# Softmax reciprocal of a band-attention layer: from VectorE's reciprocal to GpSimd's power of minus one

## The chip, the cores and the metric

The kernel runs on one core of a Trainium2 chip, in one launch. The metric is device time in microseconds: the median of the timed runs. The engines are named as in the profile: PE is TensorE's matmul, PEld its weight load, DVE VectorE, ACT ScalarE, POOL GpSimd, SP SyncE, whose queue issues most of the DMAs.

## The reference

One inference step of a one-layer streaming encoder, on 2048 prompt tokens and 64 sample tokens of width 1024, all in float32. A modulated RMS norm is followed by one input projection, whose columns feed two mixers: a gated causal convolution of 31 taps over 512 channels, and an attention of 8 heads of 64 in which every chunk of 64 frames reads its own and the 8 chunks before. Both are gated, summed, projected and added to the input; then comes a gated feed-forward of width 2816. The change is in the attention's softmax:

```python
def band_attend(q, k, v, q_pos, k_pos, rel_bias):
    s = jnp.einsum('bqhd,bkhd->bhqk', q, k).astype(jnp.float32) * ATTN_SCALE
    rel = jnp.clip(q_pos[:, None] - k_pos[None, :], -MAX_REL, MAX_REL) + MAX_REL
    s = s + rel_bias[:, rel].astype(jnp.float32)[None]
    ...
    s = jnp.where(mask[None, None], s, NEG_INF)
    p = jax.nn.softmax(s, axis=-1).astype(v.dtype)
    return jnp.einsum('bhqk,bkhd->bqhd', p, v)
```

## The kernel before

Most products are made in three passes: an operand is split into a high part and a low remainder (`hi`, `lo`; `whi`, `wlo` for weights, `hh`, `hl` for the normalised input, `ph`, `pl` for probabilities), and `mm3` (line 700) multiplies high by high, high by low and low by high.

The program has two phases. **Phase 1** (0 to about 1190 us) takes the tokens in four blocks of 576 or 512. For each block it makes q, k and v (stages "q", "k", "v"), then the gated convolution's input and the convolution (stages 0 to 3), then the gates ("g"); the norms of the next block's token tiles are made under the gates. The attention of a block starts after its "v" and runs beside the stages that follow, into the next block. **Phase 2** merges the mixers and runs the feed-forward; the change doesn't touch it.

The convolution's taps are 30 `scalar_tensor_tensor` on DVE for each channel tile and block (line 1252; `y<-u,wd,y` in the profile): output so far plus shifted input times a weight. `conv_norm` (line 1257) then normalises, with sums on POOL (`s<-s,y`, `s<-s,ln`) and a product on POOL (`y<-y,s`).

The attention of one head and block has four score tiles of 128 queries (in the first block there is one more head of 64 sample queries for each head). For a tile, PE multiplies q and k into `sc` (line 1480 or 1491). `softmax_max` (line 1350) lets DVE add the bias, take the row maximum into `sm` column 0 and copy the tile to SBUF (`pr<-sc,bias`); ACT then takes the exponentials in place, with their row sum in `sm` column 2 (`pr<-pr,sm`, and ACTIVATION_READ_ACCUMULATOR). `softmax_scale` (line 1366) makes the sum's reciprocal into `sm` column 3, and ACT multiplies the tile by it (the second `pr<-pr,sm`; `ON_ACT` on line 48 names every block). `attend` (line 1463) issues the scale of tile t-1 behind the maximum of tile t, and the scale of the last tile at the end. PE then transposes the four tiles (`ptp<-ident,pr`), ACT and DVE split the result into `ph` and `pl`, and PE multiplies by v into `po`.

What sets the order. The core's engines run in program order each. The program is written by generators (`attend`, `convolve`, `conv_norm`, `qk_rows`, `norm_tile`) in lanes, which are stepped while PE's products are issued. A small account (class `Stream`, lines 170 to 227) keeps an estimated load for each engine: a step waits until PE's load has reached the load of the engines that it depends on. `stream.after("act", "dve")` raises ACT's load to DVE's less 200 ns, and an operation adds its estimate, 83 ns for the old reciprocal and 260 ns for a power on one column. So a changed estimate moves whole steps between PE's products. A scheduler then places the instructions of each engine.

Beside the softmax, POOL already raises to a power in `rsqrt_mean` (line 722; `r<-t,mhalf`), for the norms: one column for a token tile's norm (`square`, line 1124), eight for the heads' norms of q and k (`qk_rows`). A token tile's norm runs ACT's squares (`junk`), DVE's sum and scale, POOL's power, DVE's product with the tile (`x_t<-x_t,r`), PE's transposes (`pt<-ident,x_t`).

Of the kernel before, what the change touches and what calls it, by code (L numbers as in the profile page):

```python
# [8 lines left out]
F32 = mybir.dt.float32  # L9
F32R = mybir.dt.float32r  # L10
AF = mybir.ActivationFunctionType
ALU = mybir.AluOpType
# [4 lines left out]
P = 128  # L17
# [594 lines left out]
def streaming_layer(ctx: ExitStack, tc: tile.TileContext, I, O):  # L612
    nc = tc.nc
    stream = Stream()
    pe, dve, act, gps = (
        Meter(e, n, stream) for e, n in ((nc.tensor, "pe"), (nc.vector, "dve"), (nc.scalar, "act"), (nc.gpsimd, "pool"))
    )
# [13 lines left out]
    const = ctx.enter_context(tc.tile_pool(name="const", bufs=1))  # L631
# [17 lines left out]
    dve.memset(ones, 1.0 / CONV)  # L649
    mhalf = const.tile([P, 8], F32, name="mhalf")  # L650
    dve.memset(mhalf, -0.5)
    eps_t = const.tile([P, 1], F32, name="eps_t")
    dve.memset(eps_t, EPS)

# [709 lines left out]
        return pr, sm, free, stream.when("act")  # L1364

    def softmax_scale(pr, sm, n, w, on_act):
        dve.reciprocal(sm[:n, 3:4], sm[:n, 2:3])
        if on_act:
            stream.after("act", "dve")
            act.activation(pr[:n, :w], pr[:n, :w], AF.Copy, scale=sm[:n, 3:4])  # L1370
        else:
            dve.tensor_scalar(pr[:n, :w], pr[:n, :w], sm[:n, 3:4], None, ALU.mult)

    def load_qk(x, h, q0, nq, k0, nk):
# [88 lines left out]
    def attend(i):  # L1463
# [10 lines left out]
        for t in range(0, nq, P):  # L1474
            n = min(P, nq - t)
            if x not in (0, "s"):
                ps = ps_a.tile([P, 2, 512], F32, tag="s", name="sc")
                for j in range(2):
                    for d in range(2):
                        pe.matmul(ps[:, j, :320], q2[:, d, t : t + P], kk[:, t + 320 * j : t + 320 * j + 320], start=d == 0, stop=d == 1)  # L1480
                w, src, bs = 640, ps[:, :, :320], bias[:, ::-1]
            else:
                w = nk if x == "s" else t + P

                if "banks" not in now:
                    sc = ps_a.tile([P, 2, 512], F32, tag="s", name="sc")
                    now["banks"] = [sc[:, 0:1], sc[:, 1:2]]
                ps = now["banks"].pop(0)
                now["banks"].append(ps)
                for d in range(2):  # L1490
                    pe.matmul(ps[:n, 0, :w], q2[:, d, t : t + n], kk[:, :w], start=d == 0, stop=d == 1)
                src, bs = ps[:n, 0:1, :w], bias[:n, 64:384][:, ::-1] if x == "s" else bias[:, :w][:, ::-1]
            pr, sm, free, ready = softmax_max(src, n, w, bs)
            tiles.append((pr, sm, n, w))
            if t + P < nq:
                yield free + PE_LAG, SCORE_ROOM
            else:
                fetch(i + 1)
                if (x, order[min(i + 2, len(order) - 1)][0]) in ((0, 0), ("s", "s")):
                    fetch_qk(i + 2)  # L1500
                now["scored"] = i
            if t:
                softmax_scale(*tiles[-2], x in ON_ACT)
        yield ready
        softmax_scale(*tiles[-1], x in ON_ACT)
        yield stream.when("act" if x in ON_ACT else "dve") + PE_LAG
        while now["finished"] < i - 1:
# [747 lines left out]
```

## Time and profile before

| | |
|---|---|
| timed runs | 2988.55, 2989.11, 2995.56 us; median 2989.11 |
| profiled execution | span 2982.2 us from its first to its last instruction; the page gives no other time for it |
| PE, DVE, ACT, POOL busy | 2906.6, 2047.4, 1363.6, 1165.8 us |
| phase 1, 60 to 1190 us | PE idle 28.0 us, DVE busy 850.8 of 1130 us, POOL busy 161.9 us |
| reciprocals of the softmax | 136 on DVE, from 184.4 to 1184.0 us |

How to read it: the page's groups name an instruction by engine, operation, output and inputs with shapes and the number of them, then busy time and mean, then the idle time of the engine before them and what ended it. The view of the waits adds the idle times up by what was waited for. The timeline lists start, duration and instruction, with the idle time ahead of it in brackets. A buffer of four tiles that is used in turn has one name in all of them.

### The profile page before, as it was taken

The numbers are of one execution on the slowest core, as the hardware profiler recorded it, in microseconds if no ns is written. First come the engines' busy times: TensorE is split into PE (matmuls) and PEld (weight loads), VectorE is DVE, ScalarE is ACT, GpSimd is POOL, SyncE is SP. The second block draws the span as 40 slices with busy tenths as digits, with TensorE's granted clock in tenths as the row PEclk, the third lists the DMA queues.
The fourth block names the chain that finished last, engine by engine and source line by source line (L and its number), as shares of the span: only waits on it lengthen the run. The fifth ranks groups of instructions, "written<-read, shape, count | busy, mean of one in ns | idle before, by whom it ended". The sixth has DMA issues, their size and how long they took to land. (4 is left out here: it accounts for less than half of the span.)

```text
span 2982.2 us, 44930 instructions
## 1 busy us (share of the span) xinstructions
PE 2906.6 (97%) x16241; PEld 2588.0 (87%) x16241; DVE 2047.4 (69%) x3628; ACT 1363.6 (46%) x2459; POOL 1165.8 (39%) x752
## 2 busy tenths in 40 slices
PE   7999899999999999989999999999999999999999
PEld 4899777787888888878989899999999999999998
DVE  5897687667857885477677755676666557566666
ACT  3345643662456257464443335544444345444442
POOL 0201310111011102444666443365766742465767
PEclk9999999999999999999999999999999999999999
DMA  8989889888997888885444786423333975333333
GB/s 296 304 282 306 264 286 312 279 256 276 308 283 221 281 256 277 265 284 167 139 147 149 233 268 222 135 89 113 114 106 116 308 244 184 98 96 114 114 104 126
DMA packets 467724, 628.06 MB, mean 211 GB/s; under 512 B 36276, under 2 KB 314664, under 8 KB 467501
## 3 DMA queue, kind: packets, MB, share of 16 engines
q1 hardware_dynamic: 453456, 605.58, 62.8%
q10 hardware_dynamic: 14045, 19.60, 1.9%
q8 instruction: 128, 2.10, 0.3%
q14 instruction: 95, 0.78, 0.1%
HBM read 476.53 MB, written 148.54 MB: 210 GB/s over the span
## 5 line engine op out<-in xcount | busy, mean ns | idle before, releaser
L102 PE MATMUL ps<-t,whi 128*128 128x384 f32 (+1 forms) x2112 | 502.7, 322 | 9.5 <-ACT t L102 4.9
L102 POOL TENSOR_TENSOR wlo<-wst,whi 128x1024 fp32r<-128x1024 f32 (+1 forms) x160 | 365.1, 2292 | 254.1 <-ACT whi L102 231.9
L102 ACT ACTIVATE whi<-wst 128x1024 fp32r<-128x1024 f32 (+1 forms) x264 | 257.4, 977 | 324.8 <-PE ps L102 118.5
L102 PE MATMUL ps<-b,whi 128*128 128x384 f32 (+1 forms) x1584 | 381.3, 326 | 6.1 <-DVE early L102 3.4
L102 PEld LDWEIGHTS ps<-t,whi 128*128 128x128 f32 x2112 | 367.6, 188 | 17.2 <-ACT t L102 5.1
L102 DVE SCALAR_TENSOR_TENSOR y<-u,wd,y 128x512 f32<-128x512 f32 (+1 forms) x480 | 369.1, 773 | 6.4
L102 PE MATMUL ps<-hh,whi 128*128 128x512 f32 (+2 forms) x992 | 361.3, 364 | 0.0
L102 DVE TENSOR_TENSOR acc<-acc,pd 128x512 f32<-128x512 f32 (+1 forms) x482 | 322.5, 685 | 54.9 <-PE pd L102 52.4
L102 PE MATMUL ps<-hl,whi 128*128 128x512 f32 (+2 forms) x992 | 345.2, 348 | 0.0
L102 PE MATMUL ps<-hh,wlo 128*128 128x512 f32 (+2 forms) x992 | 344.9, 348 | 0.0
L102 PE MATMUL ps<-t,wlo 128*128 128x384 f32 (+1 forms) x1056 | 339.3, 321 | 1.0 <-POOL wlo L102 0.7
L102 PE MATMUL pd<-whi,hid 128*128 128x512 f32 (+1 forms) x956 | 307.2, 391 | 0.2 <-DVE hid L102 0.2
L102 PEld LDWEIGHTS ps<-b,whi 128*128 128x128 f32 x1584 | 278.6, 189 | 12.4 <-DVE early L102 4.2
L102 POOL TENSOR_TENSOR r<-t,mhalf 128x1 f32<-128x1 f32 (+3 forms) x68 | 83.7, 1232 | 456.4 <-DVE t L102 451.3
L102 PE MATMUL ps<-b,wlo 128*128 128x384 f32 (+1 forms) x792 | 256.9, 325 | 0.0
L102 ACT ACTIVATE pr<-pr,sm 128x640 f32<-128x640 f32 (+3 forms) x272 | 200.2, 747 | 109.7 <-DVE sm L102 107.1
L102 PEld LDWEIGHTS pd<-whi,hid 128*128 128x128 f32 (+1 forms) x956 | 174.6, 183 | 42.4 <-ACT hid L102 0.7
L102 PEld LDWEIGHTS ps<-hh,wlo 128*128 128x128 f32 x992 | 186.6, 188 | 21.7
L102 PEld LDWEIGHTS ps<-hh,whi 128*128 128x128 f32 x992 | 187.2, 189 | 18.5 <-issue 1.6
L102 PEld LDWEIGHTS ps<-hl,whi 128*128 128x128 f32 x992 | 187.3, 189 | 15.5 <-issue 1.4
L102 PEld LDWEIGHTS ps<-t,wlo 128*128 128x128 f32 x1056 | 198.2, 188 | 2.6 <-POOL wlo L102 1.3
L102 POOL TENSOR_TENSOR wlo<-ws,whi 128x512 fp32r<-128x512 f32 x96 | 125.2, 1325 | 173.7 <-ACT whi L102 170.8
(227 smaller groups left out, 6307.0 us busy)
## 6 DMA issues: line engine op xcount, KB each, us to landing
whi<-w_din_h SPq DMA_DIRECT2D x72, 512.0 KB, 6.6
wlo<-w_din_l SPq DMA_DIRECT2D x72, 512.0 KB, 8.2
wst<-sum_d SPq DMA_DIRECT2D x132, 256.0 KB, 2.8
wfo<-in_w_ffn_out SPq DMA_DIRECT2D x64, 512.0 KB, 3.3
wmod<-in_w_ada SPq DMA_DIRECT2D x46, 512.0 KB, 6.2
sum_d<-ws SPq DMA_DIRECT2D x88, 256.0 KB, 2.4
wst<-in_w_ffn_in SPq DMA_DIRECT2D x84, 256.0 KB, 3.1
wst<-in_w_in SPq DMA_DIRECT2D x40, 512.0 KB, 9.1
```

What stands on the lines that cost most here:

```text
L102: self.last = f(*args, **kw)
```

## The change

A constant column of -1 is made at the start. The reciprocal becomes a power of -1 on GpSimd, and the account of loads follows it: POOL after ACT, then ACT after POOL. ACT still multiplies; the branch for a scale on DVE is not taken by any block.

```diff
     mhalf = const.tile([P, 8], F32, name="mhalf")
     dve.memset(mhalf, -0.5)
+    mone = const.tile([P, 1], F32, name="mone")
+    dve.memset(mone, -1.0)
...
     def softmax_scale(pr, sm, n, w, on_act):
-        dve.reciprocal(sm[:n, 3:4], sm[:n, 2:3])
+        stream.after("pool", "act")
+        gps.tensor_tensor(sm[:n, 3:4], sm[:n, 2:3], mone[:n], ALU.pow)
         if on_act:
-            stream.after("act", "dve")
+            stream.after("act", "pool")
             act.activation(pr[:n, :w], pr[:n, :w], AF.Copy, scale=sm[:n, 3:4])
         else:
+            stream.after("dve", "pool")
             dve.tensor_scalar(pr[:n, :w], pr[:n, :w], sm[:n, 3:4], None, ALU.mult)
```

136 reciprocals leave DVE and 136 powers come to POOL. Apart from the constant, each engine issues the same instructions as before; their order is the same up to the first attention head and again from the end of the last one, and differs between.

First place: POOL at the end of the first block's attention, where the next block's token tiles are normalised. `s<-s,ln` and `y<-y,s` belong to the convolution's norm, `wlo` to a weight, `r<-t,mhalf` 128x1 to a token tile's norm, `sm<-sm,mone` is the new power. Before:

```order
L102 TENSOR_TENSOR s<-s,ln 128x512 x3
L102 TENSOR_TENSOR wlo<-wst,whi 128x1024
L102 TENSOR_TENSOR y<-y,s 128x512 x4
L102 TENSOR_TENSOR r<-t,mhalf 128x1 x2
L102 TENSOR_TENSOR r<-t,mhalf 128x8 x4
```

And now:

```order
L102 TENSOR_TENSOR wlo<-wst,whi 128x1024
L102 TENSOR_TENSOR s<-s,ln 128x512
L102 TENSOR_TENSOR r<-t,mhalf 128x1
L102 TENSOR_TENSOR r<-t,mhalf 128x8
L102 TENSOR_TENSOR y<-y,s 128x512 x4
L102 TENSOR_TENSOR sm<-sm,mone 128x1
L102 TENSOR_TENSOR r<-t,mhalf 128x1
L102 TENSOR_TENSOR sm<-sm,mone 128x1 x2
```

The third token tile's power has moved ahead of the four products, the fourth stands behind them and one softmax power.

Second place: PE at the same point, with the last scores of that block (`sc`) and the fourth token tile's transposes (`pt<-ident,x_t`). Before:

```order
L102 MATMUL sc<-kk,q_1733 128x512 x2
L102 MATMUL ps<-whi,hh 128x512
L102 MATMUL ps<-wlo,hh 128x512
L102 MATMUL ps<-whi,hl 128x512
L102 MATMUL sc<-kk 64x320 x2
L102 MATMUL pt<-ident,x_t 128x128 x4
L102 MATMUL ps<-whi,hh 128x512
```

And now:

```order
L102 MATMUL ps<-whi,hl 128x512
L102 MATMUL sc<-kk,q_1735 128x128 x2
L102 MATMUL sc<-kk,q_1735 128x256 x2
L102 MATMUL sc<-kk,q_1735 128x384 x2
L102 MATMUL sc<-kk,q_1735 128x512 x2
L102 MATMUL pt<-ident,x_t 128x128 x2
L102 MATMUL ps<-whi,hh 128x512
```

The four score tiles now stand together, without products between them, and the sample head comes later.

Third place: DVE at the third head of the second block, from the maximum of its third tile on (ISA is that maximum and its accumulator's reading). Before:

```order
L102 ISA pr,sm<-sc,bias 128x640
L102 ISA sm 128x1
L102 SCALAR_TENSOR_TENSOR y<-u,wd,y 128x512 x2
L102 RECIPROCAL sm<-sm 128x1
L102 SCALAR_TENSOR_TENSOR y<-u,wd,y 128x512
L102 ISA pr,sm<-sc,bias 128x640
L102 ISA sm 128x1
L102 SCALAR_TENSOR_TENSOR y<-u,wd,y 128x512 x2
L102 RECIPROCAL sm<-sm 128x1
L102 SCALAR_TENSOR_TENSOR y<-u,wd,y 128x512 x5
```

And now:

```order
L102 ISA pr,sm<-sc,bias 128x640
L102 ISA sm 128x1
L102 SCALAR_TENSOR_TENSOR y<-u,wd,y 128x512 x4
L102 ISA pr,sm<-sc,bias 128x640
L102 ISA sm 128x1
L102 SCALAR_TENSOR_TENSOR y<-u,wd,y 128x512 x8
```

The reciprocals are gone from between the taps, and the run of taps behind the last tile's maximum has grown to eight.

## The prediction

> **What bounds the kernel now.** The page's first lines, cut to two, give span and PE:
>
> ```profile
> span 2982.2 us, 44930 instructions
> PE 2906.6 (97%) x16241; PEld 2588.0 (87%) x16241; DVE 2047.4 (69%) x3628; ACT 1363.6 (46%) x2459; POOL 1165.8 (39%) x752
> ```
>
> PE is busy for 97% of the span, so another engine matters only where PE waits for it. The view by stretches (start:end, length, busy time of PE, PEld, DVE, ACT, POOL, granted clock, DMA share, GB/s) shows where it can:
>
> ```profile
> 60.00:182.00 122.00, 121.69 (x711) 104.12 (x709) 99.39 (x154) 42.40 (x65) 22.34 (x18) 1.00 0.88 305
> 182.00:430.00 248.00, 231.56 (x1473) 206.51 (x1474) 187.59 (x418) 136.81 (x312) 51.28 (x42) 0.98 0.87 285
> 430.00:1190.00 760.00, 748.73 (x4076) 626.23 (x4075) 563.84 (x1075) 374.61 (x677) 88.32 (x78) 1.00 0.86 276
> 1190.00:2982.00 1792.00, 1766.54 (x9737) 1627.04 (x9735) 1166.00 (x1906) 791.00 (x1370) 999.61 (x600) 1.00 0.51 164
> ```
>
> The last stretch keeps its order and has no softmax. The change can move 182 to 1190 us, where PE is idle for 16.4 and 11.3 us. The waits of PE in phase 1 (total, times, longest) say on what:
>
> ```profile
> PE pt L102 <- DVE x_t L102: 8.9, 4, 5.7
> PE sc L102 <- DVE sm L102: 7.3, 7, 2.3
> PE pm L102 <- POOL s L102: 5.5, 4, 1.9
> PE ptp L102 <- ACT pr L102: 1.4, 3, 0.7
> PE pt L102 <- DVE kn L102: 1.4, 2, 1.2
> ```
>
> The softmax chain reaches PE in two rows: 1.4 us in which transposes wait for the scaled tile (`ptp`), and 7.3 us in which scores wait for a buffer that DVE's maximum frees (`sc`). No gain can be large; a loss has no such lid.
>
> **Term 1, DVE.** What leaves DVE, and what its idle time is worth:
>
> ```profile
> L102 DVE RECIPROCAL sm<-sm x136: 107/157/167, 184.4 to 1184.0; 128x1 f32<-128x1 f32 x128, 64x1 f32<-64x1 f32 x8
> DVE sm L102 <- ACT pr L102: 25.8, 31, 1.5
> ```
>
> 136 x 0.157 = 21.4 us of DVE's work goes, and 25.8 us in which DVE stood before a reciprocal until ACT had the sum. DVE is busy for 187.6 of 248 and 563.8 of 760 us, so nearly all of this is beside PE. On PE it can shorten only the 7.3 us: bounds 0 and -7.3. A score held by the maximum behind one reciprocal gets it 0.16 us sooner, 7 x 0.16: I take **-1.1**.
>
> **Term 2, POOL's time.** The softmax power isn't in this trace, but the norms' power has its size:
>
> ```profile
> L102 POOL TENSOR_TENSOR r<-t,mhalf 128x1 f32<-128x1 f32 x32 | 18.0, 565 | 220.2 <-DVE t L102 219.1 <-DVE sm L102 0.9 <-DMA wst<-in_w_ffn_in 0.2
> ```
>
> 136 x 0.565 = 76.8 us come to POOL, over stretches in which it is busy for 51.3 of 248 and 88.3 of 760 us. Its idle time hides them: **0**, as throughput.
>
> **Term 3, latency of each head's last tile.** Inside a head the scale of tile t-1 stands behind the maximum of tile t, and PE only comes to the transposes later. What counts is the last tile. From its score its chain is maximum, exponential, sum's reading, reciprocal, scale:
>
> ```profile
> L102 DVE CUSTOM_DVE_ANT_0 pr<-sc,bias 128x640 f32<-128x640 f32 x96 | 78.4, 817 | 32.4 <-PE sc L102 30.1 <-DMA bias<-rb_d 1.7
> L102 ACT ACTIVATE pr<-pr,sm 128x640 f32<-128x640 f32 x192 | 156.2, 825 | 65.3 <-DVE sm L102 64.0 <-ACT gate L102 0.4
> L102 ACT ACTIVATION_READ_ACCUMULATOR pr<-pr,sm 128x1 f32 x128 | 23.9, 187 | 0.0
> ```
>
> Without the reciprocal, 0.82 + 0.83 + 0.19 + 0.83 and the maximum's own reading (under 0.1) make about 2.8 us. The reciprocal adds its wait behind DVE's queue; first and last of the 136 pairs, sum's reading and reciprocal:
>
> ```profile
> 182.96 0.19 ACT L102 ACTIVATION_READ_ACCUMULATOR pr<-pr,sm 128x1 f32 x1
> 184.40 0.16 DVE L102 RECIPROCAL sm<-sm 128x1 f32<-128x1 f32 x1
> ...
> 1183.77 0.19 ACT L102 ACTIVATION_READ_ACCUMULATOR pr<-pr,sm 128x1 f32 x1
> 1183.98 0.16 DVE L102 RECIPROCAL sm<-sm 128x1 f32<-128x1 f32 x1 [1.50 <-ACT pr L102]
> ```
>
> End to end the first takes 1.41 us (184.56 less 183.15, a convolution tap in between), the last 0.18; over all 136 the mean is 1.13. An undisturbed power takes 0.57 + 0.05 for the hand-over, 0.62. So the average falls, but the tiles that the taps leave alone get 0.44 us later.
>
> POOL is not always undisturbed. Five of its operations, against like ones (1.65 for the undisturbed eight columns, 0.30 for the 128x64 sum):
>
> ```profile
> 640.62 1.65 POOL L102 TENSOR_TENSOR r<-t,mhalf 128x8 f32<-128x8 f32 x1 [4.01 <-DVE sm L102]
> 919.59 2.02 POOL L102 TENSOR_TENSOR r<-t,mhalf 128x8 f32<-128x8 f32 x1 [6.24 <-DVE t L102]
> 969.48 1.94 POOL L102 TENSOR_TENSOR r<-t,mhalf 128x8 f32<-128x8 f32 x1 [10.60 <-DVE t L102]
> 405.95 2.60 POOL L102 TENSOR_TENSOR r<-t,mhalf 128x8 f32<-128x8 f32 x1 [3.94 <-DVE t L102]
> 354.44 2.62 POOL L102 TENSOR_TENSOR r<-t,mhalf 128x8 f32<-128x8 f32 x1 [2.63 <-DVE t L102]
> 266.66 0.30 POOL L102 TENSOR_TENSOR s<-s,y 128x64 f32<-128x64 f32 x1 [31.58 <-DVE y L102]
> 230.33 4.60 POOL L102 TENSOR_TENSOR s<-s,y 128x64 f32<-128x64 f32 x1 [32.54 <-DVE y L102]
> ```
>
> They were held for 0.37, 0.29, 0.95, 0.97 and 4.30 us, 1.4 in the mean. In the longest hold DVE ran a solid row of operations on two SBUF tensors, and POOL's ended as DVE came to one that reads PSUM (`po`):
>
> ```profile
> 230.88 1.21 DVE L102 TENSOR_TENSOR wlo<-wst,whi 128x1024 fp32r<-128x1024 f32 x1
> 234.77 0.69 DVE L102 TENSOR_TENSOR o_p<-other,po 64x512 f32<-64x512 f32 x1
> ...
> 407.38 0.74 DVE L102 SCALAR_TENSOR_TENSOR y<-u,wd,y 128x512 f32<-128x512 f32 x1
> ```
>
> The tap at 407.38 ran beside the power of 405.95 and kept 0.74 us, so DVE pays nothing that I can see. The Trainium skill says more, in "SBUF — State Buffer", section "Who interferes with whom": a DVE instruction with two SBUF inputs contends with a GpSimd instruction that reads SBUF, and the loser is blocked for the other's whole instruction. By that rule DVE would lose up to 0.565 us for each power that falls into a run of taps, 37.9 us for 67 of them, more than term 1 relieves; the tap at 407.38 doesn't show it, the hold at 230.33 shows POOL's side.
>
> Now each head's margin: in the changed program's order I count PE's products between a head's last score and that tile's transposes, at 0.23 us each for 512 columns (rows 345.86 and 346.09 below), less the reciprocal's latency. Before, 2.2 to 7 us are left, and PE waits 1.4 us in all. Attention steps move in the new order, and distances shrink and grow: the very last head has 2.3 in place of 3.4, so 2.3 - 0.62 = 1.7 are left where 2.8 are needed.
>
> - POOL never held: the shortfalls add to 4.7, less the 1.4 of today: +3.3.
> - Powers that fall in a run of taps (67 of 136 by the order) held 1.4 us: 10.5 - 1.4 = **+9.1**.
> - Powers held until the whole run of taps is over (up to 4.2 us, once 8.8, third head of the second block): 30.1 - 1.4 = +28.7.
>
> I take the middle one, because four of the five holds are under 1 us, and keep both ends.
>
> **Term 4, from block 1 to block 2.** The order shown ahead moves token-tile norms here. Today:
>
> ```profile
> 340.77 0.66 PE L102 MATMUL pt<-ident,x_t 128*128 128x128 f32 x4 [1.29 <-DVE x_t L102]
> ...
> 345.86 0.39 PE L102 MATMUL ps<-wlo,hh 128*128 128x512 f32 x1
> 346.09 0.39 PE L102 MATMUL ps<-whi,hl 128*128 128x512 f32 x1
> ...
> 352.74 1.09 PE L102 MATMUL pt<-ident,x_t 128*128 128x128 f32 x4 [5.65 <-DVE x_t L102]
> ...
> 356.03 0.63 PE L102 MATMUL ps<-wlo,hh 128*128 128x512 f32 x1
> 356.46 0.63 PE L102 MATMUL ps<-whi,hl 128*128 128x512 f32 x1
> ```
>
> ```profile
> 334.80 4.62 POOL L102 TENSOR_TENSOR y<-y,s 128x512 f32<-128x512 f32 x4
> ...
> 351.25 0.55 POOL L102 TENSOR_TENSOR r<-t,mhalf 128x1 f32<-128x1 f32 x1 [11.32 <-DVE t L102]
> ```
>
> PE loses 1.29 + 5.65 = 6.9 us on `x_t`. In the new order the third tile's power leaves its place behind the 4.62 us of products, so the 1.29 should go; the fourth's stands behind those products and a softmax power. I bound the term by 0 (both waits stay) and -6.9 (both go) and take half, **-3.4**. Behind the long wait about ten products stand 0.43 apart and not 0.23, which costs 2.0 us; half of it, **-1**. The Trainium skill has this as the clock gate ("TensorE: Matmul & The Clock Gate", Part 1: half clock after an idle window of about 3.4 us, full after as long a busy one); by its figure a wait of 3.4 us may or may not bring the slow clock, and the trace agrees with its 5.65 us.
>
> **Sum.** -1.1 + 0 + 9.1 - 3.4 - 1.0 = +3.6 us on a span of 2982.2. The median of the runs lies 6.9 us above that span, and I carry this over: 2989.1 + 3.6 = about **2993**.
>
> **Rivals.**
>
> *POOL is blocked through runs of taps* (slower). The mechanism is the 4.30 us hold at 230.33, at each head's last tile. For it: the length of that hold, and POOL's end just as DVE came to a PSUM input. Against it: the four short holds. Price: 28.7 - 1.1 - 3.4 = +24, so 3013. It decides where it takes the sum past +9, so term 3 past 14.5: from +3.3 unheld to +9.1 at a hold of 1.4 us the term grows by 4.1 for each us of hold, so that is a mean hold of about 2.7 us. The skill's sentence above is this rival's rule.
>
> *The reordering alone wins* (faster). Both `x_t` waits and the slow stretch go (-8.9), the `sc` waits go (-7.3), POOL is never held (+3.3): -13, so 2976. For it: those are PE's two largest waits. Against it: most `sc` waits are at a head's start, where no reciprocal is near.
>
> *POOL's own queue*: a last tile's power behind the 4.62 us of products. The order shows powers behind them, none of a last tile, so it costs 1 to 3 us: 2996, within the forecast's range.
>
> That 136 reciprocals don't become 136 powers is excluded by the order.
>
> **How the numbers follow.** The forecast's case is everything within 9 us of the time before, 0.3%, about what a measurement of this kernel can tell from no change: chance 0.60, holding the 2996 as well. The blocked POOL has 0.32, since even half of its price passes 9 us; the winning order 0.08. The range reaches from 2980, part of the way to 2976, to 3013, the slower rival's price: the ends of term 3 with terms 1 and 4 at their bounds.
>
> **What would show it.** Right: powers `sm<-sm,mone` on POOL, 136 with a mean near 1.3 us (0.57 + 1.4 x 67/136); `ptp <- ACT pr` from 1.4 to about 10 us; `pt <- DVE x_t` from 8.9 to about 5; the tap's mean near 0.75. The slower rival: powers with a mean over 1.9 (0.57 + 2.7 x 67/136), `ptp <- ACT pr` near 30. The faster one: `ptp` under 5 with both `x_t` and `sc` near nothing. Taps that grow longer would overturn term 1; a new wait of PE in phase 1 that isn't in these rows, most of all a new place of the four tiles' norms, would overturn term 4.

## The result, and the profile after

The changed kernel takes 3013.16 us (median of 4 runs, 3011.87 to 3013.53) against 2988.83 for the kernel before on the same chip: ratio 1.0076, 95% interval 1.0059 to 1.0092. It is slower by 23 to 24 us, at the upper end of the range and at the price of the rival in which POOL is blocked. The profile shows another mechanism than that rival's. (The ratios of this document leave out one run of the kernel before, 5652 us at a granted clock of 0.936.)

The first lines of the page, after:

```profile
span 3010.1 us, 45010 instructions
PE 2915.1 (97%) x16241; PEld 2588.8 (86%) x16241; DVE 2043.4 (68%) x3493; ACT 1363.7 (45%) x2459; POOL 1248.5 (41%) x888
```

The span is 27.9 us longer than that of before. Nearly all of it lies between the first product of a score and the last product of probabilities with v; cut there, the stretch holds the same number of products in both (before, then after; columns as ahead):

```profile
181.60:1191.00 1009.40, 981.53 (x5556) 833.63 (x5554) 751.77 (x1492) 511.49 (x989) 139.60 (x120) 0.99 0.86 278
183.20:1219.10 1035.90, 994.61 (x5556) 838.16 (x5554) 741.58 (x1356) 512.63 (x988) 222.62 (x256) 0.99 0.84 271
```

The stretch is 26.5 us longer, the rest of the program 1.4. PE's idle time in it goes from 27.9 to 41.3 us, 13.4 more, and the same products keep PE busy for 13.1 us more. Part of this is the clock: by the granted clock in the traces, the stretch runs at half clock for 10.2 us before (two pieces, at 184.7 and 351.9) and for 27.3 us after (five pieces, at 185.7, 195.9, 356.3, 550.9 and 1018.5). One of them:

```profile
550.90:557.70 6.80, 4.02 (x9) 2.70 (x10) 3.36 (x6) 1.19 (x2) 1.24 (x2) 0.50 1.01 313
```

There the products of 512 columns stand 0.43 us apart and not 0.23, as in the prediction's rows. If all take twice their time, 17.1 us more of it costs some 8.5 us (an estimate); the rest of the longer busy time isn't explained here. PE's waits in phase 1, largest first:

```profile
PE ptp L102 <- ACT pr L102: 12.8, 15, 2.0
PE pm L102 <- POOL s L102: 8.0, 4, 4.9
PE sc L102 <- DVE sm L102: 6.4, 11, 1.0
PE pt L102 <- DVE x_t L102: 2.8, 3, 1.3
PE sc L102 <- DMA kk<-k_d: 2.2, 2, 1.6
```

The waits of transposes for a scaled tile have gone from 1.4 to 12.8 us, 3 to 15 of them. By their places in the heads, 11 of the 15 (8.0 us) are at a head's last tile, two (2.7) at a first and two (2.1) at a third. The waits on `x_t` have gone from 8.9 to 2.8; a wait of the convolution's sums (`pm`) has grown to 4.9 us. And the power itself, with what stood before it and who waited for it:

```profile
L102 POOL TENSOR_TENSOR sm<-sm,mone x136: 535/550/1427, 184.8 to 1212.4; 128x1 f32<-128x1 f32 x128, 64x1 f32<-64x1 f32 x8
...
L102 POOL TENSOR_TENSOR sm<-sm,mone 128x1 f32<-128x1 f32 x128 | 80.6, 630 | 403.6 <-ACT pr L102 401.9 <-DMA q<-q_d 1.8
```

```profile
ACT pr L102 <- POOL sm L102: 83.3, 101, 3.1
```

The 128 powers of 128 rows take 0.63 us in the mean; over all 136 the median is 0.55 and the longest 1.43: POOL was not blocked through runs of taps. Pairing each sum's reading with its reciprocal, the mean from the one's end to the other's end even fell, from 1.13 us to 0.87. That mean is held up by a few very late reciprocals before, 13.28 us the latest; the median rose a little, from 0.64 to 0.69. The average latency is better and the kernel slower.

Where it bites is seen in the timelines. First head of the second block, PE before (products left out), then after:

```profile
480.87 0.85 PE L102 MATMUL sc<-kk,q 128*128 128x320 f32 x4 [0.93 <-DVE sm L102]
...
482.75 0.85 PE L102 MATMUL sc<-kk,q 128*128 128x320 f32 x4 [1.03 <-DVE sm L102]
483.44 0.38 PE L102 MATMUL ptp<-ident,pr 128*128 128x128 f32 x2
```

```profile
484.91 0.85 PE L102 MATMUL sc<-kk,q 128*128 128x320 f32 x4 [0.93 <-DVE sm L102]
487.36 0.33 PE L102 MATMUL ptp<-ident,pr 128*128 128x128 f32 x1 [1.60 <-ACT pr L102]
487.45 0.83 PE L102 MATMUL sc<-kk,q 128*128 128x320 f32 x4
```

Before, the first tile's transpose stands behind the third score; after, it stands ahead of it, and PE waits 1.60 us, though DVE's maximum, which the third score needs, ended at 486.62. In blocks 2 to 4 this is the only one of 24 heads in which a transpose stands ahead of the third score. ACT and POOL at that place, after:

```profile
484.89 0.83 ACT L102 ACTIVATE pr<-pr,sm 128x640 f32<-128x640 f32 x1 [0.85 <-DVE sm L102]
485.63 0.19 ACT L102 ACTIVATION_READ_ACCUMULATOR pr<-pr,sm 128x1 f32 x1
486.48 1.55 ACT L102 ACTIVATE pr<-pr,sm 128x640 f32<-128x640 f32 x2 [0.67 <-POOL sm L102]
```

```profile
485.89 0.55 POOL L102 TENSOR_TENSOR sm<-sm,mone 128x1 f32<-128x1 f32 x1 [8.62 <-ACT pr L102]
```

ACT stands idle for 0.67 us while POOL makes the power. What it does first then is the scale, and the next tile's exponential comes behind it (one row, x2). Another head of the same block, ACT before and after:

```profile
616.80 0.83 ACT L102 ACTIVATE pr<-pr,sm 128x640 f32<-128x640 f32 x1 [0.66 <-DVE sm L102]
617.54 0.19 ACT L102 ACTIVATION_READ_ACCUMULATOR pr<-pr,sm 128x1 f32 x1
617.63 0.81 ACT L102 ACTIVATE pr<-pr,sm 128x640 f32<-128x640 f32 x1
```

```profile
629.77 0.82 ACT L102 ACTIVATE pr<-pr,sm 128x640 f32<-128x640 f32 x1
630.49 0.18 ACT L102 ACTIVATION_READ_ACCUMULATOR pr<-pr,sm 128x1 f32 x1
631.40 1.55 ACT L102 ACTIVATE pr<-pr,sm 128x640 f32<-128x640 f32 x2 [0.72 <-POOL sm L102]
```

Before, the exponential (the row with a reading behind it) waits only for its own maximum and the scale of the tile ahead runs behind it, without a wait. After, the scale comes first and waits for its power, and the exponential stands behind both. Counted by start times over the 96 neighbours of the prompt heads, the scale of tile t-1 starts ahead of the exponential of tile t 41 times before and 85 times after. So a power inside a head delays the next tile's exponential, and through it the last tile. From the start of a last tile's maximum to the end of its scale it is 3.65 us in the mean of the 32 prompt heads before and 4.24 after (medians 3.29 and 4.14).

### The profile page after: what moved, and what is told of

Read it like the earlier page. It is cut to its first block, busy times and chain, and to the rows that moved or that the text cites. A ratio compares the mean times of both kernels' runs of the same rounds, so it can differ in the third digit from the quotient of the medians.

```text
span 3010.1 us, 45010 instructions
## 1 busy us (share of the span) xinstructions
PE 2915.1 (97%) x16241; PEld 2588.8 (86%) x16241; DVE 2043.4 (68%) x3493; ACT 1363.7 (45%) x2459; POOL 1248.5 (41%) x888
## 4 chain that ended last, share of the span: by engine, by line
PE 77%; DVE 10%; ACT 4%; DMA 4%; issue 3%; POOL 2%; SPq 0%; ACTq 0%; POOLq 0%; DVEq 0%
PE ps L102 48%; PE pd L102 15%; PE pw L102 6%; DVE y L102 4%; PE po L102 2%; ACT pr L102 1%; PE ptp L102 1%; DVE wlo L102 1%; PE sc L102 1%; PE pt L102 1%; DVE pr L102 1%; POOL sm L102 1%; DMA tg<-g_d 1%; PE pa L102 1%; ACT whi L102 1%
## 5 line engine op out<-in xcount | busy, mean ns | idle before, releaser
L102 ACT ACTIVATE pr<-pr,sm 128x640 f32<-128x640 f32 (+2 forms) x272 | 199.4, 748 | 165.2 <-POOL sm L102 83.3
L102 POOL TENSOR_TENSOR sm<-sm,mone 128x1 f32<-128x1 f32 (+1 forms) x136 | 86.8, 639 | 434.2 <-ACT pr L102 432.4
L102 POOL TENSOR_TENSOR r<-t,mhalf 128x8 f32<-128x8 f32 (+3 forms) x68 | 80.3, 1184 | 304.5 <-DVE t L102 304.3
```

The lines of the kernel that those rows point to most:

```text
L102: self.last = f(*args, **kw)
```

## The experiments

The theories. **A, order**: the new account gives PE another order, and that costs. **B, latency**: the power takes longer than an undisturbed reciprocal, and that costs at each head's last tile. **C, place**, formed after the first four runs: the power costs where scales stand ahead of exponentials on ACT. All ratios are to the kernel before, run on the same chip; the last column is the row `PE ptp <- ACT pr` of each profile, total and times (for g1 two such rows together). "Before" and "after" in the second column hold but for some hundred to three hundred of PE's instructions, which stand at other places.

| kernel | PE's order | power or reciprocal | us, median | ratio, 95% interval | ptp waits, us |
|---|---|---|---|---|---|
| before | before | reciprocal | 2989 to 2991 | 1 | 1.4, 3 |
| after | after | power | 3013.16 | 1.0076 (1.0059 to 1.0092) | 12.8, 15 |
| e1 | before | power | 3013.95 | 1.0086 (1.0072 to 1.0099) | 17.0, 15 |
| e2 | after | reciprocal | 2996.63 | 1.0023 (1.0014 to 1.0032) | 0.8, 2 |
| e3 | after | power twice | 3063.36 | 1.0250 (1.0236 to 1.0264) | 44.4, 29 |
| e4 | a third | power | 3029.25 | 1.0135 (1.0120 to 1.0151) | 13.0, 12 |
| f1 | after | power, tied | 3001.66 | 1.0042 (1.0030 to 1.0054) | 4.5, 6 |
| f2 | before | power, tied | 3004.54 | 1.0052 (1.0041 to 1.0063) | 9.1, 10 |
| f3 | before | reciprocal, tied | 2989.17 | 0.9999 (0.9990 to 1.0007) | 0.8, 2 |
| h2 | after | power, last tiles reciprocal | 3011.09 | 1.0075 (1.0062 to 1.0088) | 8.0, 11 |
| g1 | before | reciprocal, scale first | 2991.86 | 1.0003 (0.9994 to 1.0012) | 1.9, 4 |
| h1 | after | power, tied, last tiles reciprocal | 3000.39 | 1.0035 (1.0023 to 1.0048) | 1.2, 3 |
| h3 | before | power, tied, last tiles reciprocal | 2993.61 | 1.0007 (0.9998 to 1.0016) | 1.5, 4 |
| d1 | after | power twice, tied | 3022.29 | 1.0113 (1.0097 to 1.0130) | 13.4, 14 |

**e1, the power in the old order.**

```diff
-        stream.after("pool", "act")
-        gps.tensor_tensor(sm[:n, 3:4], sm[:n, 2:3], mone[:n], ALU.pow)
+        stream.add("dve", "reciprocal", 1, (), {})
+        nc.gpsimd.tensor_tensor(sm[:n, 3:4], sm[:n, 2:3], mone[:n], ALU.pow)
         if on_act:
-            stream.after("act", "pool")
+            stream.after("act", "dve")
```

> The power on POOL, but entered in the account as the old reciprocal was (83 ns on DVE, ACT after DVE): PE's order is then that of before but for 154 of 16009 instructions. Theory A, the order that the new account makes costs the 24 us, and the power itself next to nothing: 2989, within 6 us of before. Theory B, the power's latency (0.70 us from the sum's reading to its end in the profile after, with the holds) in the chain of each head costs it: 3005 to 3015. The prediction's middle case would have it at +8.

Measured 3013.95: theory A falls as the main cause. With the account of before the power costs as much as the whole change. The few instructions of PE that moved are not harmless, though; at the head shown above:

```profile
495.47 0.85 PE L102 MATMUL sc<-kk,q 128*128 128x320 f32 x4 [0.93 <-DVE sm L102]
497.92 0.33 PE L102 MATMUL ptp<-ident,pr 128*128 128x128 f32 x1 [1.60 <-ACT pr L102]
```

The transpose stands behind the second score here too, and on ACT 84 of the 96 scales stand ahead of the next exponential. The account is that of before, so it is the scheduler behind it that does this. The moved products are not all of it: four waits at last tiles (at 871.4, 1060.5, 1172.0 and 1194.9, together 6.0 us) stand where PE's order is exactly that of before.

**e2, the reciprocal in the new order.**

```diff
-        gps.tensor_tensor(sm[:n, 3:4], sm[:n, 2:3], mone[:n], ALU.pow)
+        stream.add("pool", "tensor_tensor", 1, (ALU.pow,), {})
+        nc.vector.reciprocal(sm[:n, 3:4], sm[:n, 2:3])
```

> DVE's reciprocal, entered in the account as the power is (260 ns on POOL, ACT after POOL): PE's order is that of after but for 178 of 16009 instructions. Theory A: 3013, within 6 us of after. Theory B: 2989, the time before.

Measured 2996.63, some 7 us (4 to 10) above before, between both theories and nearer to B: the order costs a little, the power the larger part. On ACT only 35 of the 96 scales stand ahead, so that place comes with the power and not with the account. Its waits:

```profile
PE pm L102 <- POOL s L102: 7.8, 4, 5.0
PE sc L102 <- DVE sm L102: 7.2, 9, 1.3
PE pt L102 <- DVE x_t L102: 5.0, 2, 3.2
```

The long `pm` wait of after (4.9) is here without any power (5.0): it belongs to the order. But the order's price is hardly in waits. The stretch of the attention in e2:

```profile
182.70:1202.10 1019.40, 989.65 (x5556) 837.57 (x5554) 752.15 (x1492) 511.10 (x988) 136.66 (x120) 0.99 0.85 275
```

PE is idle for 29.8 us against 27.9 before, but busy for 8.1 us more; at half clock it runs for 20.4 us against 10.2, which is some 5 us of the 8.1 by the estimate above.

**e3, the power twice.**

```diff
-        gps.tensor_tensor(sm[:n, 3:4], sm[:n, 2:3], mone[:n], ALU.pow)
+        gps.tensor_tensor(sm[:n, 1:2], sm[:n, 2:3], mone[:n], ALU.pow)
+        nc.gpsimd.tensor_tensor(sm[:n, 3:4], sm[:n, 2:3], mone[:n], ALU.pow)
```

> After with a second power, outside the account, ahead of each one on POOL: PE's order is exactly that of after, and each scale comes 0.55 us later. Theory A: PE waits on scaled tiles 15 times in the profile after; each can grow by 0.55, so at most +8 (3013 to 3021). Theory B: the latency counts at the heads' last tiles and through ACT's queue; another 0.55 for each of 136 tiles gives as much again as the change did, +15 to +25 (3028 to 3038).

Measured 3063.36, 50 us over after: beyond both expectations. 136 x 0.55 is 75 us, so two thirds of the second power reach the end.

```profile
PE ptp L102 <- ACT pr L102: 44.4, 29, 2.6
```

The order of PE, of ACT and of DVE is the same as in after, word for word, although each scale comes 0.55 us later: the order is made as if the power took no time of note (inferred from that; the scheduler's own estimate wasn't looked at).

**e4, DVE's load kept in the account.**

```diff
-            stream.after("act", "pool")
+            stream.after("act", "pool", "dve")
```

> After, but the account lets ACT's load wait for DVE's as well as POOL's, as it did before; the power stays on POOL at 260 ns. PE gets a third order (2559 of 16009 instructions differ from before, 3485 from after). Theory A with the reason that transposes come too soon because DVE's load was dropped from the account: the waits of transposes fall from 12.8 to under 5 us, time 2985 to 3000. If any new order costs, whatever the account says: 3005 to 3020. Theory B: 3013 as after.

Measured 3029.25, above all that was expected. The row of the scaled tiles is as in after, but other waits are new:

```profile
PE ptp L102 <- ACT pr L102: 13.0, 12, 2.0
PE ps L102 <- ACT hh L102: 8.6, 1, 8.6
...
PE sc L102 <- DMA kk<-k_d: 5.6, 3, 3.4
```

The reason I gave, that DVE's load was missing in the account, is wrong. This run shows that a new order can cost 16 us more with the same powers. Its longest new wait is one step that comes late (`hh`, 8.6); how the 16 us divide wasn't followed.

**f1 and f2, the exponential first.** After and e1, with one tie:

```diff
+        now["exp"] = act.last.ins
...
-            act.activation(pr[:n, :w], pr[:n, :w], AF.Copy, scale=sm[:n, 3:4])
+            with tc.issue_after(behind) if behind else nullcontext():
+                act.activation(pr[:n, :w], pr[:n, :w], AF.Copy, scale=sm[:n, 3:4])
...
-                softmax_scale(*tiles[-2], x in ON_ACT)
+                softmax_scale(*tiles[-2], x in ON_ACT, now["exp"])
```

> After, with one tie: within a head ACT's scale of tile t-1 is issued only behind the exponential of tile t. PE's order stays that of after but for 177 of 16009 instructions. Theory C: on ACT the scale of tile t-1 now stands ahead of the exponential of tile t (85 of 96 times in the profile after, 41 of 96 before), so each exponential waits for the power ahead of it, and a head's chain grows by one power for each tile. Then the tie gives most of it back: PE's waits for scaled tiles fall from 12.8 to under 5 us, time 2990 to 3000. Theory B (the power's 0.5 us more at a head's last tile, wherever it stands): 3005 to 3013.

> The power on POOL in PE's order of before (as e1), with the same tie on ACT; PE's order differs from before in 255 of 16009 instructions. Theory C: 2985 to 2997, where e1 had 3014. Theory B: 3005 to 3014.

Measured 3001.66 and 3004.54: each about 10 us less than without the tie (0.34% in both), nearly half of the loss. f1 lies below what B expected, f2 at its lower edge, and both gave less back than C expected. In both profiles no scale starts ahead of the next exponential. PE's first transposes move back as well (at the head shown, behind four scores in the built order), so the tie takes away the pair, scale first and transpose early.

**f3 and g1, the two places with the reciprocal.** f3 is before with the tie; g1 is before with every scale of tile t-1 issued ahead of the exponential of tile t, entered in the account as before:

```diff
-    def softmax_max(ps, n, w, bias):
+    def softmax_max(ps, n, w, bias, ahead=None):
...
+        if ahead:
+            pr0, sm0, n0, w0 = ahead
+            nc.vector.reciprocal(sm0[:n0, 3:4], sm0[:n0, 2:3])
+            ins = nc.scalar.activation(pr0[:n0, :w0], pr0[:n0, :w0], AF.Copy, scale=sm0[:n0, 3:4]).ins
+        with tc.issue_after(ins) if ahead else nullcontext():
             act.activation(pr[:n, :w], pr[:n, :w], AF.Exp, bias=sm[:n, 0:1], scale=-1.0, accum_out=sm[:n, 2:3])
...
```

> Before, reciprocal on DVE, with the same tie on ACT for the 41 of 96 tiles whose scale stood ahead of the next exponential. Theory C: those gain too where the reciprocal is late behind DVE's taps, 0 to 8 us: 2981 to 2989. Theory B: no change, 2989. Slower than 2992 would say that the tie itself delays scales that PE waits for.

> Before, reciprocal on DVE, but ACT's scale of tile t-1 is always issued ahead of the exponential of tile t (before does so for 41 of 96 tiles). PE's order differs from before in 241 of 16009 instructions; the reciprocal stays 0.16 us long. Theory C (the place on ACT costs, because the exponential then waits for whatever the scale waits for): slower than before, +3 to +12, 2993 to 3002, the scale waiting for a reciprocal behind DVE's maximum and taps. Theory B (only the power's longer duration costs): no change, 2989.

Measured 2989.17 and 2991.86, no change in either. For g1 theory C's expectation missed, and B's held: all 96 scales stand ahead, the exponentials wait longer (0.97 us behind their maximum in the mean, 0.55 in after), and yet PE waits only 1.9 us for scaled tiles. With the reciprocal on DVE the transposes stand where the tiles are ready:

```profile
485.10 0.86 PE L102 MATMUL sc<-kk,q 128*128 128x320 f32 x4 [1.03 <-DVE sm L102]
485.79 0.38 PE L102 MATMUL ptp<-ident,pr 128*128 128x128 f32 x2
```

So it isn't the place on ACT alone. It costs together with a power that the order of PE leaves no time for; this much is argued from g1, f1 and e3 together, since no run puts the scale first under a power and leaves all of PE's order alone.

**h2, h1 and h3, the last tiles.** The 40 last tiles go back to DVE, in after (h2), in f1 (h1) and in f2 (h3); the account stays that of the run that each starts from. In h2 and h1:

```diff
+        if last:
+            stream.add("pool", "tensor_tensor", 1, (ALU.pow,), {})
+            nc.vector.reciprocal(sm[:n, 3:4], sm[:n, 2:3])
+        else:
             gps.tensor_tensor(sm[:n, 3:4], sm[:n, 2:3], mone[:n], ALU.pow)
```

> After, but the last tile of each head (40 of 136) has its reciprocal on DVE, in the account as the power; the other 96 stay powers on POOL. PE's order is that of after but for 144 instructions. Theory C: the exponentials still wait for the powers ahead of them, so at most a third of the loss comes back: 3003 to 3013. Theory B: the last tile is where the latency counts, so nearly all of it comes back: 2990 to 2999.

> f1 (power on POOL, new order, exponential ahead of the scale) with the 40 last tiles' reciprocals on DVE. If the tie and the last tiles are all that the power costs, only the new order is left: 2994 to 2999, as e2 (2996.6). If powers inside the heads cost more beside: 3000 to 3003, as f1.

> f2 (power on POOL, PE's order of before, exponential ahead of the scale) with the 40 last tiles' reciprocals on DVE. The powers of last tiles stand in f2 behind POOL's products and splits up to 3.9 us, and PE waited 9.1 us for scaled tiles. If that is what is left of the loss: 2987 to 2994, no longer slower than before by a measurable step; 96 powers on POOL then cost nothing. If not: 3000 to 3005, as f2.

Measured 3011.09, 3000.39 and 2993.61. h2 came as theory C expected and not as B. In the new order the last tiles are worth about 2 us by the medians, with intervals that overlap with those of after and f1, although the row of the scaled tiles falls from 12.8 to 8.0 us in h2. In the old order they are worth 0.45%, 11 to 13 us, and what is left is within 0.16% of before. In f2 POOL's own queue was in the way of some of them; the sixth head of the last block, POOL and PE:

```profile
1153.84 4.63 POOL L102 TENSOR_TENSOR y<-y,s 128x512 f32<-128x512 f32 x4 [0.87 <-DVE s L102]
1158.42 0.55 POOL L1371 TENSOR_TENSOR sm<-sm,mone 128x1 f32<-128x1 f32 x1
```

```profile
1159.89 0.33 PE L102 MATMUL ptp<-ident,pr 128*128 128x128 f32 x1 [2.03 <-ACT pr L102]
```

The sum was read at 1154.35, and the power waited 4 us for four products. In after two last tiles wait behind those products, too (2.5 us each), but PE comes later there. Two other powers of after stand 1.6 us behind other work of POOL, and PE waits for both: 1.96 us at the first head's last tile (its sum was read at 191.07) and 1.47 us at the last head's third. The first of them, POOL and PE:

```profile
191.84 0.85 POOL L102 COPY u<-hist 128x30 f32<-128x30 f32 x1
192.66 0.54 POOL L102 TENSOR_TENSOR sm<-sm,mone 128x1 f32<-128x1 f32 x1
```

```profile
194.01 0.55 PE L102 MATMUL ptp<-ident,pr 128*128 128x128 f32 x3 [1.96 <-ACT pr L102]
```

**d1, f1 with the power twice.**

```diff
-        gps.tensor_tensor(sm[:n, 3:4], sm[:n, 2:3], mone[:n], ALU.pow)
+        gps.tensor_tensor(sm[:n, 1:2], sm[:n, 2:3], mone[:n], ALU.pow)
+        nc.gpsimd.tensor_tensor(sm[:n, 3:4], sm[:n, 2:3], mone[:n], ALU.pow)
```

> f1 with each power doubled on POOL, as e3 doubled it in after, where the second 0.55 us cost 50 us. Theory C: with the exponential ahead of the scale a power no longer stands between one tile's exponential and the next, so the second one counts only at first and last tiles and costs 5 to 20: 3007 to 3022. Theory B: it costs again about 50: 3045 to 3055.

Measured 3022.29, 21 us over f1 where the same edit cost 50 over after, with PE's order as in f1. As theory C expected (at the upper end): behind the exponential a power costs less than half.

No version beats the kernel before; f3, g1 and h3 come level with it.

## Why the prediction was wrong in its likeliest case

The forecast was +3.6 us; the ratio gives +23. By the runs, the order alone is worth +7 (e2) and the power in that order +16 (after less e2, 0.53%). The two don't simply add: with the account of before the power costs +25 (e1), so under a power the new order costs nothing more that the runs can tell. The forecast had -4.4 for the order (term 4) and +8.0 for the rest.

- **Bound.** Right: 26.5 of the 27.9 us are in the attention's stretch of phase 1, and the rest of the program takes as long as before within 1.4 us.
- **Term 1, DVE.** Right: `sc` waits fell from 7.3 to 6.4 us, 0.9 against 1.1 taken; the 512-wide tap has 754 ns against 749.
- **Term 2, POOL's time.** Right as throughput: POOL stood idle for 402 us ahead of the 128 long powers alone.
- **Term 3: the step that failed.** "Inside a head the scale of tile t-1 stands behind the maximum of tile t, and PE only comes to the transposes later. What counts is the last tile." The place is half right: 11 of the 15 waits are at last tiles. But the last tile is late because powers inside the head reach it. On ACT the scale stands ahead of the next exponential in 85 of 96 cases, so that exponential waits for the power of the tile ahead; with the exponential first (f1) the waits fall from 12.8 to 4.5 us and nearly half of the loss goes. That the size of the waits, +9.1 taken, came near (12.8 less 1.4 is 11.4) is luck: it was worked out with 67 powers held for 1.4 us each, and the 136 powers were held for 0.09 us in the mean (0.64 less 0.55), 0.88 at most. The 1.4 is a mean over five operations that were held; the prediction's own rows had the norms' power of the same size, 32 with a mean of 0.565, hardly above the single one of 0.55. Nor is a wait's price on the end the wait alone. Between e2 and after the row grows by 12.0 us and the time by 16; between before and e1 by 15.6 and 25. The built order that I read for distances showed ACT's order, too; I only measured each last tile in it.
- **Term 4, the step with the wrong sign.** The `x_t` waits fell by 6.1 us, more than the 3.4 taken. But a new long wait stands elsewhere: `pm` waits 4.92 us where the convolution's taps on DVE come late against PE, and the slow clock is there (products 0.43 us apart, the piece at 550.9). POOL's sum that PE waits for, and PE:

```profile
552.54 1.09 POOL L102 TENSOR_TENSOR s<-s,y 128x512 f32<-128x512 f32 x1 [4.47 <-DVE y L102]
```

```profile
553.68 2.07 PE L102 MATMUL pm<-s,ones 128*128 128x512 f32 x2 [4.92 <-POOL s L102]
554.77 1.42 PE L102 MATMUL ps<-hh,whi 128*128 128x512 f32 x1
555.98 0.63 PE L102 MATMUL ps<-hl,whi 128*128 128x512 f32 x1
556.41 0.63 PE L102 MATMUL ps<-hh,wlo 128*128 128x512 f32 x1
```

I took one long wait away and gave no price to what is late next; a new wait stood only among the signs. In sum the waits on `x_t` and `pm` didn't grow (14.4 us before, 12.8 in e2, 10.8 after); what the order costs is PE's longer busy time, 8.1 us in the profile of e2, of which half clock is some 5. I had half clock follow the one long wait alone. In the trace of after, four of its five pieces (all but that at 550.9) begin beside waits of less than 2 us each. Why the products take the other 3 us stays open.

- **The slower rival** had the right time for a wrong reason. Its sign, a mean power over 1.9 us, isn't there (0.64 over all 136). That its price, 3013, is the measured time is luck: it was the price of holding powers, and what was paid is scales that ACT and PE meet too early, with the slow clock. Its sum also leaves out the -1.0 that the forecast's sum has. Nor does the range's upper end follow as stated: term 3 at its end with terms 1 and 4 at their bounds of 0 gives 28.7, so 3018.
- **POOL's own queue**, priced at 1 to 3 us. "None of a last tile" was wrong: two in after. Behind the four products it cost PE nothing in that order; behind other work of POOL it held two tiles for which PE waited 1.96 and 1.47 us, so the price was near, at other places than it was worked out for. In the old order it is in what h3 takes back.

What stays open: how the 16 us of the power in the new order divide. The tie takes 10 of them (0.34%); last tiles up to 2; the rest, some 3 to 4 us between h1 and e2, is within the intervals. Scale first and products moved in PE's order came together under a power on POOL, so their shares weren't told apart; a transpose ahead of the third score is seen at one head (1.60 us).

## What to carry to other kernels

An operation that moves to an idle engine takes its latency into every chain that it stands in, and the mean latency says nothing: look at what stands behind its user on each in-order engine, and at how far the next consumer is. Where a scheduler places instructions by its own estimates, compare the built order of all the engines around the moved operation, tile by tile and not only the last one. When a long wait is removed from a busy engine, look for the next late thing before the gain is booked, and look at the granted clock beside the waits: here PE's busy time grew by as much as its idle time.

## What the runs showed of the hardware

In after, a power beside a run of taps is delayed by about one tap at most, and the taps don't notice it. DVE and POOL:

```profile
546.12 5.48 DVE L102 SCALAR_TENSOR_TENSOR y<-u,wd,y 128x512 f32<-128x512 f32 x7
```

```profile
547.31 0.76 POOL L102 TENSOR_TENSOR sm<-sm,mone 128x1 f32<-128x1 f32 x1 [3.01 <-ACT pr L102]
```

Seven taps take 0.78 us each, as they do without a power (3.10 us for four at 545.22 before), and the power got through in the midst of them, 0.21 us late. The 51 powers that ran beside a tap took 0.76 us in the mean, the other 85 0.56; 32 of the 136 took over 0.7. A tap that follows another directly ends 0.78 us behind it with a power beside it (49 taps) and 0.79 without (157). One tap is not a limit, though: in f1 a power of 64 rows took 1.86 us beside taps of 606 columns, and in f2 one took 2.24 beside a 128x1024 split and such a tap. The 4.30 us hold of the prediction had 128x1024 splits among the taps; what made it so long stays open. By the sentence of the Trainium skill that the prediction quoted ("SBUF — State Buffer", section "Who interferes with whom"), one of the two would be blocked for the other's whole instruction: POOL's delay of up to one tap (0.88 us) in after agrees with it; a cost to DVE, 37.9 us by that rule, isn't there.
